# A decoder step in fp32: the scaling of the last two row tiles at the entry of the MLP, issued behind ScalarE's last split of the first two

## The chip, the cores and the metric

The kernel runs on one NeuronCore of a Trainium2 chip. The metric is the device time of one execution in microseconds (us), taken as the median of the runs. The engines are TensorE (PE in the profile; its weight loads are PEld), VectorE (DVE), ScalarE (ACT), GpSimd (POOL) and SyncE (SP, which issues DMAs).

## What is computed

One step of a decoder with one layer, in fp32: a prompt of 1024 rows of 1024 columns goes through it, and beside it a sample of 8 rows, whose attention reads a paged cache of 8192 positions each. The prompt's part that the change touches, cut to its core:

```python
xp = xp + merge_heads(fox_prompt(q, k, v, logf), sgu_prompt(u, z, w_s, b_s), g_att_out, g_sgu_out, w_o)
xp = xp + cross_attend(rmsnorm(xp, g_cross), mk, mv, w_cq, w_co)     # 4 heads, 256 memory tokens
f, conv_p = conv_ffn(rmsnorm(xp, g_ffn), zeros, w_up, conv_w, conv_b, w_down)
xp = xp + f
...
def rmsnorm(x, g):
    return x * lax.rsqrt(jnp.mean(x * x, axis=-1, keepdims=True) + EPS) * g
```

## The kernel before

**Products.** Every fp32 matrix is taken as a high and a low part. ACT writes the high part (a copy, L235, or L238 with a scale) and DVE the low part (the difference, L236 or L239). A product is three matmuls: high by high, high by low, low by high (`gemm3`, L272 to L274). `gemm3_late` does the same with the third matmul of all slices at the end: L280 and L281 for each slice of 128 columns, then all L284. A weight block comes by a DMA on SP (`wr`, L249, 4 buffers) and is split into `wh` by ACT (L235, 5 buffers) and `wl` by DVE (L236, 4 buffers). The next load of a `wr` buffer may be issued when both splits of the old one are done.

**Stages.** The prompt goes through in two halves of 512 rows, each of four tiles of 128 rows. For each half there follow the merge of the heads with its output projection, the cross attention, its output projection `w_co`, and the gated MLP. The work of the sample is put in between (gathers of the cache by POOL, L1428 and L1490; products on DVE, L1444; sums on DVE, L1448; PE matmuls, L1496).

**The seam.** It lies between the projection `w_co` and the MLP, once in each half, at about 690 and 1320 us. `out_proj` adds the residual to each tile and sums its squares on ACT (L230; a square is an ACTIVATE and an ACTIVATION_READ_ACCUMULATOR). `factor` makes the tile's factor 1/rms: an ACT instruction (L1031) and a power on POOL (L1032). Tiles 0 and 1 are scaled by ACT as soon as they are there (L1037). Tiles 2 and 3 are scaled later by `both`: tile 2 on ACT and tile 3 on DVE, in two halves of 512 columns each:

```python
for c in (slice(0, 512), slice(512, D)):
    nc.scalar.activation(y2[:, c], xt[2][:, c], AF.Copy, scale=r2)                      # L1044
    nc.vector.tensor_scalar(y3[:, c], xt[3][:, c], r3, None, op0=ALU.mult)             # L1045
```

`norm_T` then goes through the tiles in two pairs. For each pair it transposes the eight slices of 128 columns on PE into PSUM (L1124) and splits them, k0 to k7, with ACT (L238) and DVE (L239); behind the first pair come the matmuls of the first block of the MLP (`first`, that is `gemm3_late`). For the second pair it calls the delayed `both` (L1112), and has PE do eight matmuls whose result isn't used (`fill`, L1102) before the transposes.

**The cross attention.** For each head, PE transposes the keys (L1171), ACT copies them out of PSUM (L1175), PE forms the scores (L1188), DVE takes the maximum (L1190), ACT the exponential (L1196) and the scaling (L1201), PE transposes the weights (L1208), which ACT copies (L1209), and PE gathers the values (L1216). Queries are copied out of PSUM by ACT at L1234. The loads of `w_co` for the projection behind are issued while this goes on.

**What sets the order.** The program is written in an order, with priorities (`tc.high_priority()`) and a few edges: instructions traced inside `tc.issue_after(x)` are placed behind instruction x. From these a scheduler places every instruction on its engine by times that it models for itself. An edge can thus move instructions far from it, as the modelled times after it change. `newest(e)` is the last instruction traced for engine e.

Of the kernel before, what the change touches and what calls it, by code (L numbers as in the profile page):

```python
# [15 lines left out]
ENG = mybir.EngineType  # L16
# [62 lines left out]
def build(nc, tc, ctx, a, phases=None):  # L79
# [31 lines left out]
    def U(shape, dt=F32):  # L111
        n = 1
        for s in shape[1:]:
            n *= s
        t = upool.tile([P, UW], dt, tag="u", bufs=NU, name=nm("u"))[:, :n]
        if len(shape) == 3:
            t = t.rearrange("p (a b) -> p a b", b=shape[2])
        return t
# [113 lines left out]
    def split(src, h, l, scale=None):  # L232

        if scale is None:
            nc.scalar.activation(h, src, AF.Copy)  # L235
            nc.vector.tensor_tensor(l, src, h.bitcast(F32), op=ALU.subtract)  # L236
        else:
            nc.scalar.activation(h, src, AF.Copy, scale=scale)  # L238
            nc.vector.scalar_tensor_tensor(l, src, scale, h.bitcast(F32), op0=ALU.mult, op1=ALU.subtract)  # L239
# [129 lines left out]
    def newest(e):  # L369

        return next(i for i in reversed(nc.cur_bb.bb.instructions) if i.engine == e)
# [726 lines left out]
    def fill(tr, hs):  # L1098

        for k in range(8):  # L1100
            with tc.issue_after(newest(ENG.PE)):
                mmul(tr[:, :256], hs[k][:, 0:P], hs[k][:, 0:256], start=True, stop=True)  # L1102

    def norm_T(ys, g0, first):


        hs, ls = [], []
        for t0 in (0, 2):
            c = slice(t0 * P, (t0 + 2) * P)
            late = callable(ys[t0])  # L1110
            if late:
                ys[t0:] = ys[t0]()  # L1112
            for kk in range(0, 8, 2):
                if t0 == 0:
                    h2, l2 = U([P, 2, 512], F32R), U([P, 2, 512], F32R)
                    hs += [h2[:, 0, :], h2[:, 1, :]]
                    ls += [l2[:, 0, :], l2[:, 1, :]]
                tr = TR()
                if late and kk == 0:
                    fill(tr, hs)  # L1120
                with tc.high_priority():
                    for q in range(2):
                        for i in range(2):
                            nc.tensor.transpose(  # L1124
                                tr[:, (q * 2 + i) * P : (q * 2 + i + 1) * P], ys[t0 + i][:, (kk + q) * P : (kk + q + 1) * P], ident
                            )
                    for q in range(2):
                        k = kk + q
                        split(tr[:, q * 256 : (q + 1) * 256], hs[k][:, c], ls[k][:, c], scale=gp[:, g0 + k : g0 + k + 1])
                yield 0.6  # L1130
            first(hs, ls, c)
            if t0 == 0:
                yield 3
        held[0] = False
        return hs, ls


    def cross(xt, sq):
# [19 lines left out]
        def first(hs, ls, c):  # L1158
            gemm3_late([(ps[:, c], pairs(ws, d, hs, ls, c)) for d, ps in enumerate(begun)])

        hs, ls = yield from norm_T(xt, G_CROSS, first)
        r = rows_rstd(sq, 0, 4)
        rq = sm([P, 4], "rq", 2)
# [105 lines left out]
    def ffn(hf, xt, ys, late=None):  # L1269
# [6 lines left out]
        def first(hs, ls, c):  # L1276
            gemm3_late([(pv[:, c], pairs(w, hs, ls, c)) for w, pv in begun.values()])

        hs, ls = yield from norm_T(ys, G_FFN, first)
        if hf:  # L1280

# [751 lines left out]
```

## Time and profile before

| | |
|---|---|
| median of three runs | 1797.24 us (1796.32 to 1799.5) |
| the profiled execution | 1791.19 us, its span 1789.4 us |
| mean granted clock of TensorE | 0.994 |
| PE busy in the span | 1733.9 us (97%) |
| DVE, ACT, POOL busy | 1401.5, 733.0, 486.7 us |
| chain that ended last, by engine | PE 55%, DVE 8%, DMA 7%, issue 7%, ACT 2% |

The profile is of one execution, and its times (us from the start of the span) and line numbers are those of the kernel before. A row of the timeline has the start, the duration, the engine and line, the operation, what it writes and reads, and in brackets how long the engine stood idle before it and what ended that. A row of the windows has for each engine the busy time and the instructions in one stretch, then the granted clock of TensorE (1.00 is full speed), the DMA share and the rate in GB/s. Starts may come before the end of the row ahead, since an engine begins an instruction while the one before it drains.

### The profile page before, as it was taken

How to read it: one execution, taken by the hardware profiler on the slowest of the kernel's cores; microseconds unless marked ns; L12 is line 12 of the kernel's file. 1: busy time of each engine (PE TensorE's matmuls, PEld its weight loads, DVE VectorE, ACT ScalarE, POOL GpSimd, SP SyncE). 2: the span in 40 equal slices, each digit the busy share in tenths (PEclk: the TensorE clock that was granted, in tenths of full speed). 3: DMA queues.
4: the chain of work that ended last, by engine and by line, in shares of the span. 5: the costliest groups of instructions: out<-in, count | busy, mean ns of one | idle time of the engine just before them, and what ended most of it. 6: DMA issues, size and time to landing. Idle time of an engine off the chain costs nothing.

```text
span 1789.4 us, 25124 instructions
## 1 busy us (share of the span) xinstructions
PE 1733.9 (97%) x9653; PEld 1285.1 (72%) x9653; DVE 1401.5 (78%) x1733; ACT 733.0 (41%) x1374; POOL 486.7 (27%) x461
## 2 busy tenths in 40 slices
PE   8999999889999999999999999999999999999997
PEld 5887777656677667767777777766676778768875
DVE  4689658989788987989999999888885549855344
ACT  6332256466633725333333244335353333333232
POOL 1252333433123332233322222433322122102110
PEclk9999999999999999999999999999999999999999
DMA  8786788787697975779787788978879587568982
GB/s 299 302 301 231 291 325 326 252 282 247 256 399 287 360 300 202 290 286 346 285 306 310 292 316 306 374 296 344 332 284 351 211 309 251 189 260 298 359 310 80
DMA packets 157074, 521.06 MB, mean 291 GB/s; under 512 B 20874, under 2 KB 40842, under 8 KB 124186
## 3 DMA queue, kind: packets, MB, share of 16 engines
q0 software_dynamic: 57168, 341.14, 50.0%
q1 hardware_dynamic: 92874, 165.73, 26.5%
q10 hardware_dynamic: 6912, 12.59, 1.9%
q8 instruction: 76, 1.25, 0.3%
q14 instruction: 44, 0.36, 0.1%
HBM read 495.47 MB, written 23.93 MB: 290 GB/s over the span
## 4 chain that ended last, share of the span: by engine, by line
PE 55%; DVE 8%; DMA 7%; issue 7%; ACT 2%; POOL 2%; POOLq 0%; DVEq 0%; SPq 0%; ACTq 0%
PE ba L272 6%; PE ba L274 6%; PE ba L273 6%; DMA kv<-cache_v,io 5%; PE dv L1496 4%; PE bb L272 3%; PE bb L274 3%; PE bb L273 3%; DVE kv L1444 1%; PE ba L1063 1%; PE ba L1064 1%; PE ba L1065 1%; PE dv L331 1%; DMA kv<-cache_k,io 1%; DVE s L1448 1%
## 5 line engine op out<-in xcount | busy, mean ns | idle before, releaser
L235 ACT ACTIVATE wh<-wr 128x1024 fp32r<-128x1024 f32 (+2 forms) x220 | 228.8, 1044 | 443.5 <-PE ba L273 142.0
L236 DVE TENSOR_TENSOR wl<-wr,wh 128x1024 fp32r<-128x1024 f32 (+2 forms) x220 | 262.9, 1200 | 163.8 <-PE ba L274 57.6
L1428 POOL DMA_INDIRECT kv<-cache_k,io x128 | 187.3, 1464 | 599.1 <-DVE s L1448 337.0
L1444 DVE TENSOR_TENSOR kv<-kv,d 128x1024 f32<-128x1024 f32 (+1 forms) x156 | 258.0, 1681 | 28.3 <-DMA kv<-cache_k,io 28.1
L1448 DVE TENSOR_REDUCE s<-kv 128x16 f32<-128x1024 f32 (+1 forms) x156 | 258.4, 1673 | 0.0
L1490 POOL DMA_INDIRECT kv<-cache_v,io x128 | 160.4, 1253 | 249.4 <-PE dv L1496 166.3
L272 PE MATMUL ba<-u,wh 128*128 128x512 f32 x528 | 209.8, 398 | 0.0
L274 PE MATMUL ba<-u,wl 128*128 128x512 f32 x528 | 209.5, 397 | 0.0
L273 PE MATMUL ba<-u,wh 128*128 128x512 f32 x528 | 209.0, 396 | 0.5 <-DVE u L239 0.5
L272 PE MATMUL ba<-wh,u 128*128 128x512 f32 (+1 forms) x495 | 186.1, 378 | 0.9 <-ACT u L235 0.9
L273 PE MATMUL ba<-wl,u 128*128 128x512 f32 (+1 forms) x495 | 185.1, 375 | 1.3 <-DVE wl L236 1.3
L274 PE MATMUL ba<-wh,u 128*128 128x512 f32 (+1 forms) x495 | 183.4, 375 | 0.0
L1496 PE MATMUL dv<-kv,s 128*32 128x512 f32 x1024 | 127.1, 598 | 1.9 <-DMA kv<-cache_v,io 1.6
L274 PEld LDWEIGHTS ba<-u,wl 128*128 128x128 f32 x528 | 99.5, 188 | 29.0 <-issue 6.5
L272 PEld LDWEIGHTS ba<-u,wh 128*128 128x128 f32 x528 | 99.8, 189 | 26.5 <-issue 4.8
L273 PEld LDWEIGHTS ba<-u,wh 128*128 128x128 f32 x528 | 99.7, 189 | 25.3 <-issue 2.3
L272 PEld LDWEIGHTS ba<-wh,u 128*128 128x128 f32 x495 | 93.0, 188 | 25.0 <-issue 6.5
L272 PE MATMUL bb<-u,wh 128*128 128x512 f32 x272 | 108.7, 400 | 0.0
L274 PE MATMUL bb<-u,wl 128*128 128x512 f32 x272 | 108.1, 398 | 0.0
L273 PE MATMUL bb<-u,wh 128*128 128x512 f32 x272 | 107.8, 397 | 0.0
L273 PEld LDWEIGHTS ba<-wl,u 128*128 128x128 f32 x495 | 93.1, 188 | 20.1 <-DVE wl L236 1.9
L274 PEld LDWEIGHTS ba<-wh,u 128*128 128x128 f32 x495 | 92.9, 188 | 19.5 <-issue 2.5
(454 smaller groups left out, 3305.2 us busy)
## 6 DMA issues: line engine op xcount, KB each, us to landing
wr<-w_up SPq DMA_DIRECT2D x88, 512.0 KB
kv<-w_up POOLq DMA_DIRECT2D x22, 1024.0 KB
wr<-w_down SPq DMA_DIRECT2D x40, 512.0 KB
kv<-w_down POOLq DMA_DIRECT2D x11, 1024.0 KB
wr<-w_in SPq DMA_DIRECT2D x16, 512.0 KB
wr<-w_o SPq DMA_DIRECT2D x16, 512.0 KB
wr<-w_cq SPq DMA_DIRECT2D x16, 512.0 KB
wr<-w_co SPq DMA_DIRECT2D x16, 512.0 KB
```

Of the source, the lines that this page charges most:

```text
L235: nc.scalar.activation(h, src, AF.Copy)
L236: nc.vector.tensor_tensor(l, src, h.bitcast(F32), op=ALU.subtract)
L272: mmul(out, sh, mh, start=(i == 0), stop=False)
L273: mmul(out, sh, ml, start=False, stop=False)
L274: mmul(out, sl, mh, start=False, stop=(i == n - 1))
L331: mmul(ps[32 * j : 32 * j + 32, :w], xT[:, k, :] if nk == 8 else xT[:, k * 8 : k * 8 + 32], raw[:, q, j * w : (j + 1) * w], start=(k == 0) ...
L1063: mmul(pss[i], mh[k][:, tb], wh, start=(k == korder[0]), stop=False)
L1428: nc.gpsimd.indirect_dma_start(kv, None, a["cache_k"], off(kidx[:, b, ch : ch + 1]))
L1444: nc.vector.tensor_tensor(kvv[:, i : i + m, :], kvv[:, i : i + m, :], qb.unsqueeze(1).broadcast_to((P, m, 512)), op=ALU.mult)
L1448: nc.vector.tensor_reduce(s[:, ch * 4 + i : ch * 4 + i + m, :].rearrange("p k h -> p (k h)"), kvv[:, i : i + m, :].rearrange("p k (h d) -> ...
L1490: nc.gpsimd.indirect_dma_start(kv, None, a["cache_v"], off(kidx[:, b, ch : ch + 1]))
L1496: mmul(dv[32 * j : 32 * j + 32, :], s[:, ch * 4 : ch * 4 + 4, :].rearrange("p k h -> p (k h)"), kvv[:, j, :], start=(ch == 1), stop=(ch == ...
```

## The change

In `norm_T` the call of the delayed `both` is put inside an edge: what it traces is issued behind the newest instruction of ACT, which there is the last split of the first pair (L238 for k7).

```diff
             late = callable(ys[t0])
             if late:
-                ys[t0:] = ys[t0]()
+                with tc.issue_after(newest(ENG.Activation)):
+                    ys[t0:] = ys[t0]()
```

The lines behind it move down by one, so L1175 of before is L1176 of the changed kernel, and so on; the text uses the numbers of before. The scheduler's order changes at the seams and between them, and not before the first.

ACT at the first seam, before. Here `u_6338` is the buffer of the last two slices, k6 and k7 (its second L238 is the last split), `fac_1257` and `fac_1258` are the factors of tiles 2 and 3, and `u_6373` is the scaled tile 2:

```order
L238 ACTIVATE u_6338<-bb_6340,gp 128x256
L1031 ACTIVATE fac_1257_6279<-sqx_5897,part_5898 128x1
L1044 ACTIVATE u_6373<-u_4762,fac_1257_6279 128x512 x2
L230 ACTIVATE junk_6277,sqx_5897<-u_4764 128x512
L238 ACTIVATE u_6338<-bb_6340,gp 128x256
L1031 ACTIVATE fac_1258_6282<-sqx_5897,part_5898 128x1
L230 ACTIVATE junk_6285,ssu_5123<-u_5806 128x512
L230 ACTIVATE junk_6287,ssu_5123<-u_5806 128x512
```

and in the changed kernel:

```order
L238 ACTIVATE u_6338<-bb_6340,gp 128x256
L1031 ACTIVATE fac_1257_6279<-sqx_5897,part_5898 128x1
L230 ACTIVATE junk_6277,sqx_5897<-u_4764 128x512
L1031 ACTIVATE fac_1258_6282<-sqx_5897,part_5898 128x1
L230 ACTIVATE junk_6285,ssu_5123<-u_5806 128x512
L238 ACTIVATE u_6338<-bb_6340,gp 128x256
L1044 ACTIVATE u_6373<-u_4762,fac_1257_6279 128x512 x2
L230 ACTIVATE junk_6287,ssu_5123<-u_5806 128x512
```

The two L1044 have moved behind the last split; the square and the factor of tile 3 and one square of the sample have moved ahead of it.

ACT at the second seam, before. The buffers `u_11036`, `u_11047`, `u_11058` and `u_11069` hold k0 and k1, k2 and k3, k4 and k5, k6 and k7; `wh_11391` is a weight block of the MLP (the rows begin with the third split of the eight):

```order
L238 ACTIVATE u_11058<-ba_11060,gp 128x256
L238 ACTIVATE u_11036<-ba_11038,gp 128x256
L238 ACTIVATE u_11069<-ba_11071,gp 128x256
L238 ACTIVATE u_11047<-bb_11049,gp 128x256
L238 ACTIVATE u_11058<-ba_11060,gp 128x256
L238 ACTIVATE u_11069<-ba_11071,gp 128x256
L235 ACTIVATE wh_11391<-wr_11388 128x1024
L230 ACTIVATE junk_11018,sqx_10655<-u_9515 128x512
L1031 ACTIVATE fac_2074_11023<-sqx_10655,part_10656 128x1
L1044 ACTIVATE u_11104<-u_9515,fac_2074_11023 128x512 x2
L230 ACTIVATE junk_11021,sqx_10655<-u_9517 128x512
L1031 ACTIVATE fac_2075_11026<-sqx_10655,part_10656 128x1
```

and in the changed kernel:

```order
L230 ACTIVATE junk_11018,sqx_10655<-u_9515 128x512
L1031 ACTIVATE fac_2074_11023<-sqx_10655,part_10656 128x1
L238 ACTIVATE u_11036<-ba_11038,gp 128x256
L238 ACTIVATE u_11047<-bb_11049,gp 128x256
L235 ACTIVATE wh_11391<-wr_11388 128x1024
L238 ACTIVATE u_11036<-ba_11038,gp 128x256
L238 ACTIVATE u_11058<-ba_11060,gp 128x256
L238 ACTIVATE u_11069<-ba_11071,gp 128x256
L230 ACTIVATE junk_11021,sqx_10655<-u_9517 128x512
L238 ACTIVATE u_11047<-bb_11049,gp 128x256
L1031 ACTIVATE fac_2075_11026<-sqx_10655,part_10656 128x1
...
```

Tile 2's square and factor now stand ahead of all splits, the weight block behind the splits of k0 and k2, tile 3's square and factor between the other splits; k5, k7 and then the two L1044 follow.

ACT and DVE in the cross attention of the second half, the difference around one place. `t_1955` holds the copied keys of a head, `wr_10854` is the first block of `w_co`, split into `wh_10857` by ACT; `wl_10659` is the low part of the block whose `wr` buffer that load takes over:

```order
 L1201 ACTIVATE u_10370<-u_10370,cr_10372 128x256 x4
+L235 ACTIVATE wh_10857<-wr_10854 128x1024
 L1234 ACTIVATE u_10331<-bb_10398 128x512
 L1175 ACTIVATE t_1955_10443<-ba_10438 128x512
 L1209 ACTIVATE u_10449<-ba_10450 128x512
 L1209 ACTIVATE u_10449<-bb_10456 128x512
-L235 ACTIVATE wh_10857<-wr_10854 128x1024
```

DVE there, before:

```order
L1408 TENSOR_SCALAR d_2001_10623<-rmask,d_2001_10623 128x512
L1413 TENSOR_TENSOR tot_10741<-d_2001_10623,lfz 128x8
L1190 TENSOR_REDUCE cmx_10368<-ba_10383 128x2
L1444 TENSOR_TENSOR kv_10168<-kv_10168,d_1841_9748 128x1024 x2
L236 TENSOR_TENSOR wl_10659<-wr_10657,wh_10660 128x1024
```

and in the changed kernel:

```order
L1191 TENSOR_REDUCE cmx_10368<-ba_10373 128x2
L1191 TENSOR_REDUCE cmx_10368<-ba_10383 128x2
L1409 TENSOR_SCALAR d_2001_10623<-rmask,d_2001_10623 128x512
L236 TENSOR_TENSOR wl_10659<-wr_10657,wh_10660 128x1024
L1445 TENSOR_TENSOR kv_10168<-kv_10168,d_1841_9748 128x1024 x2
```

On ACT the split of the weight block now stands ahead of the copies of the queries, the keys and the attention weights; on DVE the low part of the earlier block has moved ahead of a pair of products of the sample and behind both maxima and a scan.

## The prediction

> **What bounds the kernel now.** I read the page first, for the engine that fills the span.
>
> ```profile
> span 1789.4 us, 25124 instructions
> PE 1733.9 (97%) x9653; PEld 1285.1 (72%) x9653; DVE 1401.5 (78%) x1733; ACT 733.0 (41%) x1374; POOL 486.7 (27%) x461
> ```
>
> PE is busy 1733.9 of 1789.4 us, so 55.5 us are left in the whole program, and an edit can pay or cost only in two ways: by a wait of PE, or by PE's own pace. ACT, which the change reorders, is at 41% and matters only where PE stands waiting for it. So the second view is PE's waits from 640 to 1360 us, which takes in both seams and the stretch between them.
>
> ```profile
> engine line waited for: us in total, times, longest us
> PE bb L1124 <- ACT u L1044: 1.7, 1, 1.7
> ...
> PE ba L1124 <- ACT u L1044: 0.7, 1, 0.7
> ```
>
> The tiles that the change delays (L1044) are waited for once at each seam, 1.7 and 0.7 us. That is the most the two named waits can give back. The third view is the windows, for the granted clock (PEclk); the first three rows are consecutive, and so are the last two.
>
> ```profile
> 690.80:694.20 3.40, 1.44 (x8) 1.00 (x8) 2.08 (x5) 2.29 (x7) 0.57 (x1) 1.00 1.01 426
> 694.20:697.60 3.40, 2.49 (x10) 2.20 (x11) 1.45 (x4) 2.86 (x9) 0.72 (x2) 0.50 1.01 419
> 697.60:701.00 3.40, 3.40 (x18) 3.40 (x17) 1.68 (x4) 0.00 (x0) 0.83 (x1) 0.50 0.52 203
> ...
> 1175.50:1178.90 3.40, 1.71 (x13) 1.38 (x12) 3.40 (x8) 1.25 (x3) 0.27 (x1) 1.00 1.01 398
> 1178.90:1182.30 3.40, 3.40 (x12) 2.82 (x11) 3.40 (x6) 0.08 (x1) 0.92 (x1) 0.50 0.24 99
> ```
>
> The first number is the length, the second PE's busy time, and the number after POOL's is the clock. After a stretch in which PE was busy 1.44 or 1.71 of 3.40 us the clock is 0.50 for the next stretch. So a loose stretch is paid twice: its wait, and then up to half of 3.4 us, **1.7 us**, in the stretch behind it. At seam 1 it is half for two stretches, since the first of them was itself loose (2.49).
>
> **Part 1, seam 1 (first half of the rows).** PE's rows there, then ACT's and POOL's:
>
> ```profile
> 694.62 0.48 PE L1124 MATMUL bb<-cp,u 128*128 128x128 f32 x1 [1.70 <-ACT u L1044]
> 695.59 0.58 PE L280 MATMUL ba<-u,wh 128*128 128x256 f32 x1 [0.49 <-ACT u L238]
> 696.18 1.91 PE L284 MATMUL ba<-u,wh 128*128 128x256 f32 x8
> ```
> ```profile
> 692.26 0.28 ACT L1031 ACTIVATE fac<-sqx,part 128x1 f32<-128x1 f32 x1
> 693.23 1.33 ACT L1044 ACTIVATE u<-u,fac 128x512 f32<-128x512 f32 x2 [0.69 <-POOL fac L1032]
> 694.47 0.61 ACT L230 ACTIVATE junk<-u 128x512 bf16<-128x512 f32 x1
> 695.08 0.45 ACT L238 ACTIVATE u<-bb,gp 128x256 fp32r<-128x256 f32 x1
> 695.44 0.28 ACT L1031 ACTIVATE fac<-sqx,part 128x1 f32<-128x1 f32 x1
> 695.62 0.61 ACT L230 ACTIVATE junk<-u 128x512 bf16<-128x512 f32 x1
> ```
>
> The last split (L238 at 695.08) is the one PE needs at 695.59. In the changed order L1044 no longer stands ahead of it, but a square (L230), tile 3's factor (L1031) and a further square do. From starts in these rows: a square takes 0.61 to the next start (694.47 to 695.08), or 0.74 where its accumulator is followed by another square; an L1031 takes 0.18 (695.44 to 695.62). Behind the L1031 at 692.26 the split then starts at 692.26 + 0.18 + 0.61 + 0.18 + 0.74 = 693.97, which is **1.1 us earlier**. POOL's 0.69 us drops out, as ACT no longer waits for the factor there. The transpose at 694.62 filled part of the old wait and must now come later; it costs 0.2. Gain **0.9 us**, between 0.5 (if a square waits for its rows) and 1.1. What is late next is L1044: it would end at 693.97 + 0.35 + 1.33 = 695.7, but behind L280 at 694.5 PE has L281 and eight L284 (1.91 us at this half clock, half that at full) before it needs the new rows, so that wait is covered; without this cover it would cost the same 1.3 us. L1045 on DVE moves earlier and hides behind L284 as well. The half clock I leave as it is: the loose stretch up to 694.2 is not removed.
>
> **Part 2, seam 2 (second half).** ACT's rows before, and PE's:
>
> ```profile
> 1321.49 0.47 ACT L238 ACTIVATE u<-ba,gp 128x256 fp32r<-128x256 f32 x1 [1.78 <-PE ba L1124]
> 1321.86 0.47 ACT L238 ACTIVATE u<-bb,gp 128x256 fp32r<-128x256 f32 x1
> ...
> 1324.79 1.06 ACT L235 ACTIVATE wh<-wr 128x1024 fp32r<-128x1024 f32 x1 [0.23 <-PE bb L1082]
> ```
> ```profile
> 1324.61 0.36 PE L280 MATMUL ba<-u,wh 128*128 128x256 f32 x1
> ...
> 1326.35 0.28 PE L280 MATMUL ba<-u,wh 128*128 128x256 f32 x1
> ...
> 1328.24 0.33 PE L1124 MATMUL ba<-cp,u 128*128 128x128 f32 x1 [0.67 <-ACT u L1044]
> ...
> 1330.66 0.17 PE L1614 MATMUL ms<-cp,mT 8*8 8x8 f32 x1 [0.51 <-DVE s L1483]
> ```
>
> The eight slices of 128 columns are called k0 to k7; PE's L280 and L281 for a slice need its L238. Here all eight splits were done before wh_11391 (the L235 at 1324.79), and PE ran its L280 to the last pair at 1326.35 without a wait. The changed order puts wh_11391 behind only two of the eight splits. It still waits for PE's last matmuls of the output projection (the 0.23 that its row names), because its buffer is read until then, and PE has the same work ahead of that, so wh_11391 again starts at 1324.79 and gives ACT free at 1325.75, 0.1 before its end. Then come, by starts 0.37 apart: k1 1325.75, k4, k6, a square 1326.84, k3 1327.58, the factor, k5 1328.1, k7 1328.5, done 1329.0. PE can use k0 from 1324.61 to about 1324.95, waits about 1.25 for k1, does k1 and k2 in 0.5, waits about 1.4 for k3, and starts k7 at 1329.1 instead of 1326.35: 2.75 us late. Against this, waits behind it vanish, since L1044 and the DVE work are done meanwhile: 0.67 for L1044 and 0.51 for L1483. Loss 2.75 − 0.67 − 0.51 = **1.6 us**. Bounds: 2.1 if only the 0.67 goes; −0.7, a gain, if ACT is not held at wh_11391 at all.
>
> The two waits make 2.65 us within 1324.95 to 1328.05. Any 3.4-us stretch that holds 1.6 us of them is as loose as the one at 1175.50. Sliding a stretch of 3.4 us over them, its start may lie from 1323.6 to 1326.05, so for 2.45 of 3.4 us, 7 in 10, if the stretches lie anyhow. Then the dense work behind runs at half clock: **1.7 us**, which I take; the ends are 0 and 3.4 (two stretches, as at seam 1).
>
> The Trainium skill, page "TensorE: Matmul & The Clock Gate", table of recommendations, names idle gaps of PE over about 3 us as what throttles the clock mid-kernel. By it the 1.25 and 1.4 us here would cost no clock, and the sum would be 1.7 us lower. The 3.40-us row at 690.80 speaks against it, as its longest single gap is 1.70 us and the half clock came. The same page, Part 1, says that the window is free-running, with 3413 ns, which fits the lengths of these rows.
>
> **Part 3, what the scheduler moved between the seams.** Most moved rows are hidden under matmuls that wait for nothing: the view of PE's waits names none in the up-projections, so their reordered copies stay covered (without cover each is a copy, some 0.6 us by L1175's row below); POOL and SP keep their order but for two factors beside gathers and one weight load behind two small transfers. One place is not hidden, in the cross attention of the second half:
>
> ```profile
> 1239.64 3.72 PE L1188 MATMUL ba<-t,u 128*128 128x256 f32 x16 [0.77 <-ACT t L1175]
> ```
> ```profile
> 1239.01 0.58 ACT L1175 ACTIVATE t<-ba 128x512 f32<-128x512 f32 x1
> ...
> 1243.67 1.06 ACT L235 ACTIVATE wh<-wr 128x1024 fp32r<-128x1024 f32 x1 [3.11 <-DMA wr<-w_co]
> ```
> ```profile
> 1235.00 0.37 SPq L249 DMA_DIRECT2D wr<-w_co  x1
> ```
> ```profile
> 1231.44 2.35 DVE L1444 TENSOR_TENSOR kv<-kv,d 128x1024 f32<-128x1024 f32 x2
> 1233.71 1.22 DVE L236 TENSOR_TENSOR wl<-wr,wh 128x1024 fp32r<-128x1024 f32 x1
> ```
>
> wh_10857 (1243.67) stood behind L1175 and waited 3.11 us for its weights at no cost. Now it stands ahead of the copies L1234, L1175 and L1209, and PE has nothing but L1188 to do. At the least L1188 is late by wh's own turn, 1.06 less the overlap at its start: 1.0 us. Its load is also issued earlier. SP issues it when DVE has ended L236 of the buffer before; that L236 ended at 1234.93 and the load went at 1235.00. With the pair L1444 moved behind L236 (and a scan of 1.2 us ahead of it), I put the end at 1233.1, 1.9 us earlier. ACT reaches wh_10857 at 1238.6, 5.5 us after that issue. The old load took 1243.67 − 1235.00 = 8.67 us beside gathers. At 1233.1 the queues are idle:
>
> ```profile
> DMA  9899599120000000000009985449999799798889
> ```
>
> These are 40 slices of 0.2 us from 1231 on: nothing moves from 1232.8 to 1235. A load issued there starts alone and I take it as landed in time, by the nearest state, the idle one: **+1.1 us** for L1188. The other end is 8.67 us again, a landing at 1241.8, and L1188 at 1241.8 + 1.04 + 0.5 + 0.58 = 1243.9, **+4.2 us**. A gain is excluded, as an instruction is put ahead of the one waited for.
>
> **Sum.** −0.9 + 1.6 + 1.7 + 1.1 = **+3.5 us**. Against its own time, the profiled execution (1791.19 us, of which 1.8 lie outside the span) would become 1794.7. It is 6 us below the median of the three times, so I add the same sum to the median: 1797.24 + 3.5 = 1800.7, said as **1800.8**. The case's own range is +1.8 to +5.2.
>
> **Rivals.** *The clock at seam 1 comes back early* (not slower). From 694.20 to 701.00 the half clock costs about half of 6.4 us, 3.2 us. If the wait at 694.2 to 695.6 goes, the stretch 694.20 to 697.60 may be dense enough for full clock behind it (1.7 back), and if the stretches lie otherwise in a run, the loose one can be split in two of which neither is loose (3.2 back). It decides whether PE's busy time in the first stretches reaches 2.5 or so of 3.4. Then −0.9 − 3.2 + 1.6 + 1.1 = −1.4: 1795.8; with a free clock at seam 2 and its ACT less held, below −3.6. For it: the change removes some 1.5 us of idle time there. Against: the stretch 690.80 stays loose.
> *No half clock behind seam 2* (within 0.2%). The two waits are split by work, and if the stretches lie so that neither holds 1.6 us of them, or 1.25 and 1.4 us are each too short to count, the 1.7 falls: −0.9 + 1.6 + 1.1 = +1.8: 1799.0. For it: 3 in 10 positions. Against: 1175.50, where 1.7 us were enough. The rule of the Trainium skill on long gaps, named above with its page, leads here too.
> *The load of w_co lands late* (slower). 4.2 in place of 1.1, and a loose stretch of 4 us with 1.7 of half clock: −0.9 + 3.3 + 4.2 + 1.7 = +8.3: 1805.5. For it: gathers start at 1235, and 8.67 us beside them. Against: the idle slices.
> *Only the seams' waits move* (the change as meant): −1.7 − 0.7 = −2.4: 1794.8, if the squares and wh_11391 find room. The order of ACT at seam 2 speaks against it.
>
> **How the numbers follow.** A measurement of this kernel tells 0.2%, about 3.6 us, from no change. Forecast 0.42, half of it within 0.2% and half slower; the clock at seam 1 0.17, of which 0.12 within and 0.05 faster; no half clock behind seam 2 0.13, all within; the late load 0.14, all slower; the change as meant 0.06, of which 0.04 within and 0.02 faster; something else 0.08, of which 0.05 slower and 0.03 faster. Sums: faster 0.05 + 0.02 + 0.03 = 0.10, slower 0.21 + 0.14 + 0.05 = 0.40, within 0.50. The range reaches from the early clock (1795.8) to the late load (1805.5), with 0.8 and 1.0 more for the bounds of parts 1 and 2: 1795.0 to 1806.5.
>
> **What would show it.** Seam 1: the last split starts about 1.1 us sooner after tile 2's factor, and no wait for L1044 is left. Seam 2: two waits of PE for L238 of 1.2 to 1.4 us around one L235, and a clock of 0.50 behind them. Cross attention: the wait before this L1188 is 1.8 us, not 0.8. I am wrong if wh_11391 starts well before PE's last L1083, if the clock stays at 1.00 behind seam 2, or if w_co is awaited ahead of L1188.

## The result, and the profile after

The changed kernel takes 1799.6 us (median of 20 runs, 1794.99 to 1805.12), the kernel before in runs on the same chips 1793.83 us (20 runs, 1788.59 to 1799.5). The ratio is **1.0037, with a 95% interval of 1.0027 to 1.0046**: 0.37% slower, about 6 us. The median of before that the prediction started from, 1797.24 us, was that of the first three of these runs. The profiled execution took 1795.76 us, 4.6 us more than the one of before, with this head of the page:

```profile
span 1793.8 us, 25129 instructions
PE 1733.0 (97%) x9653; PEld 1283.5 (72%) x9653; DVE 1399.7 (78%) x1733; ACT 732.8 (41%) x1374; POOL 488.4 (27%) x461
```

PE's busy time is what it was (1733.9 before), so the 4.4 us of span are, on balance, time in which it stood idle. PE's waits from 640 to 1360 us say which; lines behind 1112 are one higher in this kernel. The first row is from the same view of before, the others are of the changed kernel:

```profile
PE ba L280 <- ACT u L238: 1.6, 4, 0.6
```
```profile
engine line waited for: us in total, times, longest us
PE ba L280 <- ACT u L238: 6.6, 6, 2.0
...
PE ba L1189 <- ACT t L1176: 2.1, 1, 2.1
...
PE bb L1189 <- DVE u L236: 1.7, 1, 1.7
PE ms L1626 <- DVE pn L1623: 1.0, 1, 1.0
```

The waits for the delayed scaling (L1044) are gone. Those of the tile `ba` for the splits (L238) are 6.6 us, where they were 1.6: 2.8 more at seam 1 and 2.1 more at seam 2. The longest for the key copy (L1176) is 2.1, not 0.8, and the last two lines are new.

Where it came and went shows when one follows the same PE instruction through both executions. The last column is its start after, less its start before; the matmuls are named by before's lines:

```text
instruction                                   before     after    difference
L280, first of seam 1                         689.24    688.47      -0.8
L280, first of the second pair, seam 1        701.91    699.86      -2.0
L1063, projection w_o of the second half     1117.10   1114.05      -3.0
L1208, ahead of the copies, cross attention  1237.84   1233.19      -4.6
L1216, second head's values                  1253.90   1252.28      -1.6
L1081, first of the projection w_co          1296.53   1294.74      -1.8
L280, first of seam 2                        1324.61   1323.97      -0.6
L280, first of the second pair, seam 2       1332.76   1335.46      +2.7
end of the span                              1789.4    1793.8       +4.4
```

Seam 1 gains 1.3 us up to the second pair. This 1.3 holds a difference of the clock: before has half clock there from 694.22 on, for 6.8 us, and this execution has none. The cross attention takes back **3.0**, seam 2 **4.5**.

The steps between have other causes. Of the 1.0 from seam 1 to the next stage, 0.5 is the order of the matmuls right behind; further on, a wait for a gather is 0.9 longer (2.5 and 1.6 us), and a wait of 1.3 for DVE near 1110 us (L943 for L239) is gone. The 1.6 behind these is the half clock at 1178.91 (3.4 us), which only before has. Of the last step, 0.7 is a longer wait for a weight block near 1540 us (L235, 1.7 us after, 0.9 before) and 0.7 a wait for a DMA near 1585 us that is new; no wait names the rest.

Seam 1 after, PE and then ACT:

```profile
691.65 0.39 PE L280 MATMUL ba<-u,wh 128*128 128x256 f32 x1 [0.57 <-ACT u L238]
...
693.74 0.39 PE L280 MATMUL ba<-u,wh 128*128 128x256 f32 x1 [1.59 <-ACT u L238]
...
699.86 0.39 PE L280 MATMUL ba<-u,wh 128*128 128x256 f32 x1 [1.97 <-ACT u L238]
```
```profile
691.50 0.28 ACT L1031 ACTIVATE fac<-sqx,part 128x1 f32<-128x1 f32 x1
...
693.24 0.45 ACT L238 ACTIVATE u<-bb,gp 128x256 fp32r<-128x256 f32 x1
693.59 1.33 ACT L1044 ACTIVATE u<-u,fac 128x512 f32<-128x512 f32 x2
...
698.97 0.84 ACT L238 ACTIVATE u<-ba,gp 128x256 fp32r<-128x256 f32 x2 [2.71 <-DVE u L239]
```

The split now follows tile 2's factor by 1.74 us (693.24 − 691.50), where it was 2.82 (695.08 − 692.26). But PE has a new wait of 1.97 us, at the second pair. The split that it needs stands 2.71 us on ACT for a low part on DVE (L239, at 698.45), and DVE does four other scalings before that (L678, from 696.86). These belong to the gating branch of the prompt (`sgu_prompt`), as do the squares `ssu`, which were taken above for those of the sample.

The cross attention after, PE, ACT, SP and then DVE:

```profile
1236.29 3.72 PE L1189 MATMUL ba<-t,u 128*128 128x256 f32 x16 [2.06 <-ACT t L1176]
...
1250.45 1.99 PE L1189 MATMUL bb<-t,u 128*128 128x256 f32 x8 [1.67 <-DVE u L236]
```
```profile
1234.23 1.04 ACT L235 ACTIVATE wh<-wr 128x1024 fp32r<-128x1024 f32 x1
1235.18 0.57 ACT L1235 ACTIVATE u<-bb 128x512 f32<-128x512 f32 x1
1235.66 0.58 ACT L1176 ACTIVATE t<-ba 128x512 f32<-128x512 f32 x1
```
```profile
1229.09 0.37 SPq L249 DMA_DIRECT2D wr<-w_co  x1
```
```profile
1247.43 2.36 DVE L1445 TENSOR_TENSOR kv<-kv,d 128x1024 f32<-128x1024 f32 x2 [4.62 <-DMA kv<-cache_k,io]
1249.71 0.68 DVE L236 TENSOR_TENSOR u<-bb,u 128x512 fp32r<-128x512 f32 x1
```

The weight block (1234.23) had its data in time: no bracket, 5.1 us after the issue. It costs its own turn. A second wait is new: DVE stands 4.62 us for a gather of the sample, and the split that PE needs (L236 at 1249.71) is queued behind. Here is the same pair of products before, and then the issue of its gather on POOL, before and after:

```profile
1247.26 2.36 DVE L1444 TENSOR_TENSOR kv<-kv,d 128x1024 f32<-128x1024 f32 x2 [0.89 <-DMA kv<-cache_k,io]
```
```profile
1237.52 1.68 POOL L1428 DMA_INDIRECT kv<-cache_k,io  x1 [1.65 <-DVE s L1448]
```
```profile
1237.36 2.82 POOL L1429 DMA_INDIRECT kv<-cache_k,io  x1 [5.25 <-DVE s L1449]
```

PE's matmuls around it have come 4.6 us forward, but the gather is issued at the same time, and so it ends at the same time. POOL waits for the sum on DVE (L1448) that frees the buffer. That sum ended at 1237.25 before and at 1237.09 after, as the changed order puts a further pair of products (1232.50) and a weight split (1234.75) ahead of it.

Seam 2 after, ACT, DVE and then PE:

```profile
1324.14 1.06 ACT L235 ACTIVATE wh<-wr 128x1024 fp32r<-128x1024 f32 x1 [1.14 <-PE bb L1083]
1325.11 1.18 ACT L238 ACTIVATE u<-ba,gp 128x256 fp32r<-128x256 f32 x3
1326.17 0.63 ACT L230 ACTIVATE junk<-u 128x512 bf16<-128x512 f32 x1
...
1326.79 0.48 ACT L238 ACTIVATE u<-bb,gp 128x256 fp32r<-128x256 f32 x1
```
```profile
1323.91 1.22 DVE L236 TENSOR_TENSOR wl<-wr,wh 128x1024 fp32r<-128x1024 f32 x1 [0.76 <-PE bb L1082]
1325.06 0.68 DVE L1015 TENSOR_TENSOR u<-bb,u 128x512 f32<-128x512 f32 x1
```
```profile
1323.37 0.51 PE L1082 MATMUL bb<-wl,u 128*128 128x512 f32 x1
...
1325.62 0.39 PE L280 MATMUL ba<-u,wh 128*128 128x256 f32 x1 [1.17 <-ACT u L238]
...
1327.32 0.58 PE L280 MATMUL ba<-u,wh 128*128 128x256 f32 x1 [0.96 <-ACT u L238]
...
1335.22 0.43 PE L1626 MATMUL ms<-lps,ones 128*128 128x64 f32 x2 [1.03 <-DVE pn L1623]
```

PE waits 1.17 for k1 and 0.96 for k3, as ACT has the weight block and tile 3's square in between. On DVE, too, a weight split and tile 3's residual (L1015) stand among the splits; both depend on PE's last matmuls of the projection (L1082 at 1323.37). These come only 0.75 us earlier than before (1324.13), where the projection's first came 1.8 us earlier. The rest went to the sixteen matmuls of the sample (L1496), here before and after:

```profile
1321.71 1.93 PE L1496 MATMUL dv<-kv,s 128*32 128x512 f32 x16
```
```profile
1319.09 1.90 PE L1497 MATMUL dv<-kv,s 128*32 128x512 f32 x10
...
1322.38 1.06 PE L1497 MATMUL dv<-kv,s 128*32 128x512 f32 x6
```

In one row they took 1.93 us; with the transposes put in after ten of them they take 1.90 and 1.06, which is 1.0 more. The clock, in consecutive stretches at this seam:

```profile
1320.36:1323.77 3.41, 3.41 (x22) 1.79 (x21) 0.77 (x2) 1.18 (x4) 1.55 (x3) 1.00 1.00 386
1323.77:1327.18 3.41, 1.42 (x9) 0.87 (x7) 3.27 (x8) 3.04 (x8) 0.97 (x1) 1.00 0.98 377
1327.18:1330.60 3.42, 3.28 (x15) 3.29 (x16) 3.16 (x8) 2.21 (x6) 0.56 (x1) 0.50 0.87 339
```

The stretch with 1.42 us of busy PE is followed by one at half clock. No single gap in it is over 1.2 us, so the rule of the Trainium skill on gaps of over about 3 us ("TensorE: Matmul & The Clock Gate", its table of recommendations) did not hold here either.

### The profile page after: what moved, and what is told of

It reads as the page before. It is cut to its first block, busy times and chain, and to the rows that moved or that the text cites. A ratio compares the mean times of both kernels' runs of the same rounds, so it can differ in the third digit from the quotient of the medians.

```text
span 1793.8 us, 25129 instructions
## 1 busy us (share of the span) xinstructions
PE 1733.0 (97%) x9653; PEld 1283.5 (72%) x9653; DVE 1399.7 (78%) x1733; ACT 732.8 (41%) x1374; POOL 488.4 (27%) x461
## 3 DMA queue, kind: packets, MB, share of 16 engines
q8 instruction: 76, 1.25, 0.3%
## 4 chain that ended last, share of the span: by engine, by line
PE 60%; issue 8%; DVE 7%; DMA 3%; ACT 2%; POOL 2%; POOLq 0%; DVEq 0%; SPq 0%; ACTq 0%
PE ba L272 8%; PE ba L274 8%; PE ba L273 8%; PE dv L1497 5%; PE bb L272 4%; PE bb L274 4%; PE bb L273 4%; DMA kv<-cache_v,io 1%; PE ba L1063 1%; PE ba L1064 1%; PE ba L1065 1%; PE dv L331 1%; PE dv L1773 1%; PE ba L1082 1%; PE ba L1081 1%
## 5 line engine op out<-in xcount | busy, mean ns | idle before, releaser
L235 ACT ACTIVATE wh<-wr 128x1024 fp32r<-128x1024 f32 (+2 forms) x220 | 228.7, 1044 | 459.3 <-PE ba L273 139.0
L236 DVE TENSOR_TENSOR wl<-wr,wh 128x1024 fp32r<-128x1024 f32 (+2 forms) x220 | 262.8, 1200 | 169.7 <-PE ba L274 60.8
L1491 POOL DMA_INDIRECT kv<-cache_v,io x128 | 164.7, 1287 | 244.9 <-PE dv L1497 165.0
L273 PE MATMUL ba<-u,wh 128*128 128x512 f32 x528 | 208.5, 395 | 0.5 <-DVE u L239 0.5
L273 PE MATMUL ba<-wl,u 128*128 128x512 f32 (+1 forms) x495 | 185.3, 375 | 1.3 <-DVE wl L236 1.3
L273 PEld LDWEIGHTS ba<-u,wh 128*128 128x128 f32 x528 | 99.2, 188 | 25.2 <-issue 2.3
L273 PE MATMUL bb<-u,wh 128*128 128x512 f32 x272 | 107.8, 396 | 0.0
L273 PEld LDWEIGHTS ba<-wl,u 128*128 128x128 f32 x495 | 93.1, 188 | 20.0 <-DVE wl L236 1.9
```

Of the source, the lines that this page charges most:

```text
L273: mmul(out, sh, ml, start=False, stop=False)
L1491: nc.gpsimd.indirect_dma_start(kv, None, a["cache_v"], off(kidx[:, b, ch : ch + 1]))
```

## The experiments

The theory after these traces: seam 1 gains a little, and the loss is made by what the scheduler moved behind it, in the cross attention and at seam 2. Rival: the delayed scaling at seam 2 costs by itself. First a fact of the programs: with the edge at the second seam alone, the order on all five engines is that of before, row for row. All that changed comes from the edge at seam 1, or from both together.

Two numbers of each profile are given below beside the time, both from the kind of table above: **cross**, how much the shift grows from the L1208 at 1237.84 to the L1216 at 1253.90, and **seam 2**, from the L1081 at 1296.53 to the L280 at 1332.76. The changed kernel has +3.0 and +4.5. They hold the half clocks of their execution, so differences under about 1.7 us say little. Ratios are to before, in runs on the same chip.

**1. The edge at seam 1 alone.**

```diff
-                with tc.issue_after(newest(ENG.Activation)):
+                seams.append(0)
+                with tc.issue_after(newest(ENG.Activation)) if len(seams) == 1 else nullcontext():
                     ys[t0:] = ys[t0]()
```

> The edge at the first seam alone; the second call of the delayed scaling is left without one. ScalarE still has the weight block wh_11391 ahead of six of the eight splits at seam 2, now with the two L1044 ahead of k3 as well. Theory (the loss comes from the blocks that the scheduler moved after seam 1: wh_11391 at seam 2, wh_10857 in the cross attention): slower than before by 4 to 9 us, at or above the changed kernel. Rival (the delayed scaling at seam 2 is itself what costs): faster than before by 1 to 3 us, as only seam 1's gain is left.

Measured: 1.0039 (1.0023 to 1.0055), cross +3.8, seam 2 +5.1. The rival fell: without the edge at seam 2 the loss is the same, within the intervals. The whole change is the edge at seam 1 and its consequences.

**2. The weight block at seam 2 behind the splits** (the change, with one edge more).

```diff
+                lastk[:] = [newest(ENG.Activation)]
                 with tc.issue_after(newest(ENG.Activation)):
                     ys[t0:] = ys[t0]()
...
-                        w_, pv = wload(a["w_up"][ft], 1024), BK()
+                        with tc.issue_after(lastk[0]) if hf and ft == 2 else nullcontext():
+                            w_ = wload(a["w_up"][ft], 1024)
+                        pv = BK()
```

> The change with one edge more: the split of the weight block wh_11391 is placed behind the last split of seam 2 (k7), everything ahead of seam 2 as in the changed kernel. Theory: PE's two waits of about 1 us for L238 at seam 2 go and the half clock behind them mostly too, so 3 to 5 us less than the changed kernel, that is 0 to 3 us above before; what is left is the cross attention's 2 to 3 us less seam 1's gain. Rival (the delayed scaling at seam 2 costs): as the changed kernel, 5 to 7 us above before.

Measured: 1.0052 (1.0035 to 1.0069), seam 2 +4.7. This was a miss: nothing came back. Its PE, ACT and DVE rows at seam 2 say why:

```profile
1328.23 0.58 PE L280 MATMUL ba<-u,wh 128*128 128x256 f32 x1 [1.99 <-ACT u L238]
```
```profile
1327.09 0.63 ACT L230 ACTIVATE junk<-u 128x512 bf16<-128x512 f32 x1 [1.38 <-DVE u L1015]
```
```profile
1325.23 1.22 DVE L236 TENSOR_TENSOR wl<-wr,wh 128x1024 fp32r<-128x1024 f32 x1 [0.76 <-PE bb L1082]
1326.37 0.68 DVE L1015 TENSOR_TENSOR u<-bb,u 128x512 f32<-128x512 f32 x1
```

With the block out of the way, ACT stands at tile 3's square instead, which waits for the residual on DVE, which waits behind a weight split for PE's last projection matmuls. The two waits of about 1 us became one of 2.

**3. Tile 3's square and factor behind the splits as well, and alone** (two kernels, second half only). In the first, the edge of 2 stays; in the second it is off:

```diff
         def both(r2, r3):
+            if late[0]:
+                ssq_into(sq[:, 3, 1:2], xt[3][:, 512:])
+                r3 = factor(3)
...
-                    residual(xt, sq, i, n, ps)
+                    residual(xt, sq, i, n, ps, not (late[0] and i == 3))
```

> The change with, in the second half, the weight block wh_11391 and also tile 3's square and factor behind the last split of seam 2, so that no instruction of ScalarE that needs PE's last projection matmuls stands among the eight splits. Theory (either of the two holds ScalarE, which is why moving the block alone gave nothing back): the wait of 2.0 us for k3 and the half clock behind it go, seam 2 costs at most 1 us against before, 3 to 5 us less than with the block alone behind, 2 to 5 us above before in all. Rival (the first splits come too late, as the transposes have moved behind other work of PE): no gain, 6 to 9 us above before.

> The change with tile 3's square and factor alone behind the last split in the second half; the weight block stays ahead of six splits. Theory: PE's wait for k1 (about 1.1 us) stays and that for k3 (about 1 us) goes, so 1 to 3 us less than the changed kernel, 3 to 6 us above before. Rival (the square alone holds ScalarE and the block is harmless): as with both behind. Rival (neither matters): as the changed kernel, 6 to 7 us above before.

Measured: 1.0029 (1.0011 to 1.0047) with both behind and 1.0038 (1.0022 to 1.0053) with the square alone; seam 2 +4.9 and +3.2. The first lies inside the theory's time, but not by its mechanism: the wait for k3 did not go. The second is a miss: by the medians it is 6.3 us above before where 3 to 6 were expected, and PE still waits 1.16 us for k1 and 0.52 for k3. ACT and DVE of the first kernel, and then PE:

```profile
1326.68 0.47 ACT L238 ACTIVATE u<-bb,gp 128x256 fp32r<-128x256 f32 x1 [1.96 <-DVE u L239]
```
```profile
1324.24 1.23 DVE L236 TENSOR_TENSOR wl<-wr,wh 128x1024 fp32r<-128x1024 f32 x1 [0.76 <-PE bb L1089]
1325.38 0.68 DVE L1015 TENSOR_TENSOR u<-bb,u 128x512 f32<-128x512 f32 x1
```
```profile
1327.21 0.38 PE L280 MATMUL ba<-u,wh 128*128 128x256 f32 x1 [1.96 <-ACT u L238]
...
1333.37 0.38 PE L1133 MATMUL bb<-cp,u 128*128 128x128 f32 x1 [1.74 <-DVE u L1052]
```

PE still waits 2.0 us. Now it is DVE: the second split of a PSUM tile on ACT waits for DVE's low part of the first (L239), and that stands behind the weight split and the residual. And tile 3, scaled later, is itself waited for (1.74). So four instructions in two queues (the weight block and the square on ACT, the weight split and the residual on DVE) tie the splits to PE's last projection matmuls; taking one away leaves the next. The theory "the block or the square" was too narrow.

**4. The projection's last matmuls ahead of the transposes.** If that is it, the cure is on PE: let the projection end first.

```diff
+        if callable(ys[2]):
+            ends2.append(newest(ENG.PE))
...
+                            with tc.issue_after(ends2[1]) if t0 == 0 and len(ends2) == 2 else nullcontext():
                                 nc.tensor.transpose(
```

> The change with an edge on TensorE at seam 2: the transposes of the first two tiles stand behind the last matmul of the projection w_co, so that the projection ends some 4 us earlier than in the changed kernel; the edges on ScalarE are those of the change, and the cross attention is as in the changed kernel. Theory (seam 2 loses because the projection's last two matmuls stand behind the transposes and the sample's matmuls, while what depends on them stands among the splits: wh_11391 and tile 3's square on ScalarE, wl and tile 3's residual on VectorE): PE's waits for L238 at seam 2 fall to 1 us or less, the seam costs at most 1 us against before, and the whole is 1 to 3.5 us above before. Rival (the delayed scaling itself costs at seam 2): as the changed kernel, 5 to 7 us above before.

Measured: **1.0014** (1.0003 to 1.0024), seam 2 **+0.5**, cross +4.2. PE's waits from 1230 to 1340 us in this kernel:

```profile
PE ba L1192 <- ACT t L1179: 2.2, 1, 2.2
PE bb L1192 <- DVE u L236: 2.1, 1, 2.1
PE ba L280 <- ACT u L238: 1.0, 3, 0.6
...
```

The theory held in time and place: the block and the square stand among the splits still (the block ahead of all eight), and they cost little, as what they wait for is done. Of the fall from +4.5 to +0.5, about 0.8 us has another source: the L1496 stand as eight and eight here (1.07 us each) and not as ten and six. What is left is the cross attention, whose two waits are those of the changed kernel.

**5. The cross attention.** The first `w_co` block of the second half goes behind the copies of the attention weights (L1209): in the change, in the change with 2, in the change with 4, in the change with the edge at seam 1 alone, and in before.

```diff
         turned(0)
+        turn0.append(newest(ENG.Activation))
...
-                ws[kk] = wload(wpair(w, kk, n * 512, 512), 1024)
+                with tc.issue_after(turn0[1]) if ys is not None and len(turn0) == 2 and n == 0 and kk == 0 else nullcontext():
+                    ws[kk] = wload(wpair(w, kk, n * 512, 512), 1024)
```

> The change with another edge: the split of the first w_co block (wh_10857) of the second half is placed behind the copies of the first head's attention weights (L1209). The scheduler then puts wh_11391 ahead of all eight splits at seam 2. Theory: the wait for L1175 in the cross attention is back at 0.8 us from 2.1, 1 to 3 us gained, and seam 2 still waits for wh_11391, by about as much: 3 to 6 us above before. Rival (the second wait in the cross attention, of PE for the split L236, is set by a gather and not by this block): 1 us at most is gained there, 5 to 7 us above before.

> The change with both edges, so that neither block stands ahead of what PE waits for. Theory: seam 1's gain of 1 to 3 us is left and nothing is lost: 1 to 3 us below before, 6 to 9 us below the changed kernel. Rival (the reordered rest of the program costs, not these two blocks): still 2 to 5 us above before.

> The change with the w_co block behind the copies of the attention weights and with the transposes of seam 2 behind the projection's last matmul. Theory: both losses gone, PE's waits for L238 at seam 2 at 1 us or less: 0 to 2.5 us below before. Rival (seam 1's gain is too small to be told from nothing): within 1 us of before.

> The edge at seam 1 alone, with the first w_co block of the second half behind the copies of the attention weights. To be read against the next kernel, which has the same but no edge at a seam. Theory: seam 1's edge by itself is worth 1 to 3 us, as PE's wait for the last split comes 1 us sooner and the half clock ends sooner. Rival (what seam 1 gains is lost again where PE meets the stream of gathers): both kernels within 0.7 us of each other.

> The kernel before with only the first w_co block of the second half placed behind the copies of the attention weights; no edge at a seam. Theory (in the cross attention of before that block stood in nobody's way): within 2 us of before. Rival (the order that comes with it, with all blocks of the queries' weights behind the copies, is better by itself): 2 to 4 us below before, and the recovery seen with that edge was not the repair of the change's loss.

```text
kernel                           ratio to before (95%)          cross   seam 2
change + edge                    0.9993 (0.9980 to 1.0006)      -0.6     +1.4
change + edge + 2                1.0010 (0.9992 to 1.0029)      -0.4     +0.8
change + edge + 4                0.9995 (0.9980 to 1.0010)      -0.2     +1.3
edge at seam 1 + edge            1.0000 (0.9985 to 1.0015)      -0.7     +1.9
before + edge                    1.0011 (0.9997 to 1.0025)      -0.8     +2.0
```

PE's waits of the first of these, from 1230 to 1340 us:

```profile
PE ba L1218 <- ACT u L1211: 1.6, 1, 1.6
PE ba L280 <- ACT u L238: 1.5, 2, 0.8
PE bb L1218 <- ACT u L1211: 0.6, 1, 0.6
PE ba L1190 <- ACT t L1177: 0.3, 1, 0.3
```

Both new waits of the cross attention are gone, the one for the key copy (0.3) and the one for the split. One edge far from the seams takes back all of the loss; expected were 1 to 3 us, and a time 3 to 6 us above before, so this too was a miss, on the good side. The edge also changes the order that the scheduler gives to seam 2, where PE then ends the projection ahead of most transposes, as in 4. With that order, mending seam 2 besides (the second and third row) adds nothing that can be told. Of what is left at seam 2 in these rows, about 1.0 us is the L1496 again, which stand as four and twelve (1.05 and 1.91 us) or, in the third row, as two and fourteen. The rival of the gather fell too, but not cleanly: the edge also moves DVE's sums ahead of the weight splits, so the gathers are issued earlier (the one that went at 1237.36 in the changed kernel goes at 1235.57). By the waits in the profile, 1.3 of the 3.0 us are the block's and 1.7 the gather's; no experiment parts them. The last two rows differ by the edge at seam 1 alone: 0.11% less with it, which the intervals do not tell from nothing. All of them lie within 0.2% of before. The expectation for the change with 2 (1 to 3 us faster) missed, and for the change with 4 the theory and its rival can't be told apart.

**6. A smaller edge.** The `w_co` block goes only behind the key copy (L1175); ACT's order at seam 2 is then that of before.

```diff
         keys(2)
+        key2.append(newest(ENG.Activation))
...
+                with tc.issue_after(key2[1]) if ys is not None and len(key2) == 2 and n == 0 and kk == 0 else nullcontext():
```

> The change with the split of the first w_co block of the second half behind the copy of the third head's keys (L1175) only. ScalarE's order at seam 2 is then that of before (all eight splits, the weight block, tile 2's square, factor and scaling), and the splits of the queries' last weights stand behind the key copy. Theory: neither the cross attention nor seam 2 loses, seam 1's gain is left: 0 to 2.5 us below before. Rival (other reordering between the seams costs too): 2 us or more above before.

> The kernel before with only the edge of the fastest version, the first w_co block of the second half behind the copy of the third head's keys; no edge at a seam. ScalarE's order at seam 2 is then one with the weight block and tile 3's square among the splits, unlike the fastest version's. Theory (the fastest version gains by seam 1 and by keeping the order of before at seam 2): within 2 us of before, 2 to 5 us above the fastest version. Rival (the edge on the w_co block is the whole gain): 3 us or more below before, as the fastest version.

Measured: with the change, **0.9981 (0.9971 to 0.9991)**, the fastest version here: median 1790.13 us beside 1793.54 for before on the same chip; cross +0.1, seam 2 +0.9. That is 3.4 us, somewhat more than the 0 to 2.5 expected. In the kernel before, with no edge at a seam: 0.9999 (0.9980 to 1.0018). So the edge on the block isn't the gain by itself. These two kernels differ in the order of ACT at seam 2 as well as at seam 1, so the gain is not shown to be seam 1's. PE's longest waits of the fastest version, from 1230 to 1340 us:

```profile
PE ba L1190 <- ACT t L1177: 0.9, 2, 0.5
...
```

No line of that view is over 1 us. Its profiled execution was the slowest of its twelve (1794.87 us, with 6.8 us of half clock from 616.1 on and again from 698.0), so where its 0.19% come from is not read from it.

## Why the prediction was right, and where not

The time lay in the range and the sign of the sum was right: +3.5 us were forecast and about 6 measured. That 1800.8 came out at 1799.6 is partly luck: the start was 3.4 us too high (the median of three runs, 1797.24, where twenty give 1793.83), and the sum was too low by 2 to 3. By the prediction's own bound of 0.2% the result is slower; slower had 0.40, less than no change with 0.50. Point by point:

- **Seam 1** held in what was worked out: the last split came 1.08 us sooner after the factor (1.1 was said), and no wait for L1044 is left. But the gain of 1.3 us (0.9 was said) is no proof, as the clocks differ. Take PE's time from the first L280 (689.24) to the L273 at 709.31, where both orders have done the same matmuls. Without the edge, a profile with 3.4 us of half clock at the seam is 0.9 us shorter there than before with its 6.8 (two kernels, in 5 and 6). With the edge, three profiles with 6.8 us of half clock gain 0.6 to 0.8, four with 3.4 gain 1.8 to 1.9, and four with none 1.8. So at the same clock the edge is worth 0.6 to 0.9 us in the profile. On the chip that is too small to be told from nothing (0.11% between two kernels, 5).
- **The rival that the clock at seam 1 comes back early** did come in this execution, and it is chance. Of eleven profiles with the changed seam 1 seven show a half clock that begins between 692 and 698 us, the others none. The free-running window of the Trainium skill ("TensorE: Matmul & The Clock Gate", Part 1) agrees: the same code meets it at another place in each execution. The rival's price of 3.2 us was too high: against 6.8 us of half clock, none at all gives back 1.0 to 1.2, and against 3.4 us nothing. PE then waits 1.97 us for the split of the second pair instead (699.86), a wait that the prediction does not have.
- **Seam 2's waits** held in size and place: 1.17 and 0.96 us where 1.25 and 1.4 were worked out. The half clock behind them, given 7 in 10, came in all five profiles of kernels that have these waits (the changed kernel, 1, 2 and both of 3). Two costs were put at nothing, so the seam cost 4.5 us and not 3.3. One is the new wait of 1.03 for L1623. The other lies in the words "PE has the same work ahead of that": the work is the same, but the L1496 are split in two, which is 1.0 of the 1.2 us that were gone by the first L280 already (shift −1.8 to −0.6).
- **The cause named at seam 2 was too narrow.** The step "the changed order puts wh_11391 behind only two of the eight splits" is true of the order, but the block alone doesn't hold the seam: 2 and 3 showed tile 3's square, the residual and the weight split on DVE behind it, and 4 the common cause, the projection's last matmuls behind the transposes on PE.
- **The cross attention** held for the first wait: 2.06 us against 0.77, that is +1.3 (1.1 was said), and the load was issued early and landed in time. The term was too small: DVE's wait for the gather, with a split queued behind it, added 1.7. The prediction had followed ACT's queue there, and DVE's only as far as the load.
- **The late load** did not come, nor a gain at both seams.

## What to carry to other kernels

An ordering edge in a program whose order a scheduler works out acts far from its place: here the edge's own seam gained 1 us or less, and two places some 550 and 630 us behind lost 7.5 in the profile. Compare the orders of the whole program, and for each instruction that moved ahead of something PE needs, ask on every queue, VectorE's too, what it waits for, and which instruction frees the buffer of each gather that is waited for. If several queued instructions depend on the same late producer, moving one of them shows only the next; move the producer. And before a gain at one place is read from two profiles, compare their clocks there.

## What was not expected of the hardware

- A half clock needs no long gap: 1.42 us of busy PE in 3.41 us, in pieces with gaps of at most 1.2 us, was enough, and 1.96 of 3.41 us at seam 1 in the same execution (below) was not. The busy time alone doesn't settle it: 2.02 of 3.41 us was enough in before (349.47 to 352.88 us), and 1.46 was not in the change with 4 and the edge of 5 (777.41 to 780.82).

```profile
692.29:695.70 3.41, 1.96 (x16) 1.96 (x17) 1.41 (x4) 3.21 (x10) 0.68 (x2) 1.00 1.04 434
```

- Executions of one kernel spread over some 10 us (1788.59 to 1799.5 before), more than the change itself; one half clock is up to 1.7 us of it, by the 3.41 us of each at half rate, and nothing where PE would have waited anyway, as at seam 1.
- The sixteen matmuls of the sample (L1496, 32 columns of weights each) cost more when their row is broken up: 1.93 us in one row, 1.90 and 1.06 as ten and six, 1.05 and 1.91 as four and twelve, but 1.07 and 1.07 as eight and eight.
